# A decoder step's shared-value projection laid out by tokens, and two operand preparations moved, on one Trainium2 core

## The chip, the cores and the metric

The program runs on one core of one Trainium2 chip. A core has TensorE (PE: matrix products into the accumulation memory PSUM), VectorE (DVE), ScalarE (ACT), GpSimd (POOL), and SyncE (SP), which here only issues DMA transfers. Each engine works through its own instruction stream in order, and the streams meet through semaphores. The metric is the device time of one execution in microseconds (us); lower is better. Runs of one kernel are told by their median.

## The reference, cut to what matters

A two-layer decoder step over 512 prompt tokens and 32 sample tokens (8 sequences of 4), model width 1024, 8 heads of 128. Layer 0 is feed-forward, gated token mixing, feed-forward, gated embedding. From its output one shared key, value and log-forget are made, and layer 1 attends to them. All data are float32.

```python
def shared_kv(h, kv_norm, w_kvf, b_f, k_norm):
    xs = rmsnorm(h, kv_norm)
    kvf = xs @ w_kvf                                   # 1024 -> 1024 keys, 1024 values, 8 forgets
    k = rmsnorm(kvf[..., :D_ATT].reshape(bsz, L, N_HEADS, HEAD_DIM), k_norm)
    v = kvf[..., D_ATT:2 * D_ATT].reshape(bsz, L, N_HEADS, HEAD_DIM)
    logf = jax.nn.log_sigmoid((kvf[..., 2 * D_ATT:] + b_f).astype(jnp.float32))
    return k, v, logf
...
# layer 1
h = h + 0.5 * swiglu(rmsnorm(h, ffn1_norm[1]), ...)
xn = rmsnorm(h, mix_norm[1])
q = rmsnorm((xn @ att_w_q).reshape(bsz, L, N_HEADS, HEAD_DIM), q_norm)
o = fox_prompt(q, k, v, lf)          # causal softmax attention with a forget bias
h = h + o.reshape(bsz, L, D_ATT) @ att_w_o
h = h + 0.5 * swiglu(rmsnorm(h, ffn2_norm[1]), ...)
```

The keys, values and forgets are outputs too.

## The kernel before, in words

**Layout.** The activations lie transposed: features on the 128 partitions, all 544 tokens (512 prompt, then 32 sample) along the free dimension. A 1024-wide activation is 8 tiles of 128 x 544.

**Products in two parts.** Each float32 operand is split into a high part, which ACT casts (L192 for weights, L279 and L291 for activations), and a low part, which DVE subtracts (L193, L280, L292). A product is three TensorE matmuls: high x high, high x low, low x high (L235, L239, L241). In `mm` the weight block of 128 x 128 is the stationary operand and the 544 tokens move past it in two column ranges of 256 and 288, so one output tile of 128 features takes 8 blocks x 3 products x 2 ranges = 48 matmuls. The outputs go to the PSUM pool `ps`, three buffers of two banks; a second pool `pb` has two buffers of one bank. The large SBUF pool `big` has 45 buffers.

**Weights.** They come in pieces of 512 KB in a fixed order (`build` lists them). `unit` hands out the next piece and calls `prepare`, which splits up to two pieces ahead and loads up to four ahead; the load is issued on SP (L159) and the two split instructions go to ACT and DVE.

**Shared keys and values (`kv`).** One tile for the forgets; eight key tiles (evicted with the row scale `rstd` on DVE, squared on ACT L702, summed by heads with small float32 matmuls L710, then rsqrt on ACT L334 and DVE L337 to L341); then eight value tiles. The row scales of the keys go through DRAM (L721) and come back spread over the partitions (L726). Beside each value tile stand: its eviction on DVE (L765), its store (L766), the `v_turn` of the tile before (four float32 transposes L796 of 128 tokens and one for the sample tokens L797, then split and two stores L802, L803), a key's norm (`k_norm`), and `prep` of one tile of the next feed-forward's input. After value tiles 3 and 5 stands one `forms`.

**`forms`** makes four operands of the feed-forward's seven-product scheme from two input tiles: two ACT scalings (L301), three DVE differences (L305, L307, L308) and two splits (L279, L280), each waiting for the one before. The feed-forward takes four of them; those that are not there yet it makes itself beside its first four plain tiles.

**Projection after attention.** The output projection has its first half of the tokens done in `project_half` (L1172 to L1176, beside the heads), then `project(0)` to `project(7)` for the second half: 24 matmuls of 272 columns each, an add on DVE (L1196) and `on_chunk`, which makes the next input's `prep` and square, and, with `early=2`, a `forms` after chunks 1 and 3.

**Order.** In these two stages a scheduler at build time orders each engine's stream by its own time model, by the order in which the program names the steps where nothing else decides; in the feed-forward the order is written out by hand.

Of the kernel before, what the change touches and what calls it, by code (L numbers as in the profile page):

```python
# [22 lines left out]
F32 = mybir.dt.float32  # L23
# [6 lines left out]
P = 128  # L30
# [36 lines left out]

G_FFN1, G_MIX, G_FFN2, G_PLE = 0, 16, 32, 48
# [3 lines left out]
C_ID, C_ROLE, C_B4, C_H, C_SEL, C_NEGQ, C_TRI4 = 0, 128, 140, 144, 152, 156, 160  # L72
NCONST = 192
# [15 lines left out]
class Builder:  # L89
# [456 lines left out]
    def next_norm(self, h, gcol, early=0):  # L546
# [3 lines left out]
        def on_chunk(c, cols=slice(0, T)):  # L550
# [6 lines left out]
            if c % 2 and c // 2 < early and cols.stop == T:  # L557
                box["f"].append(self.forms(h, gcol, c // 2, self.pairs(box)))
        return on_chunk, box

# [170 lines left out]
    def kv(self, h, box, ffn_gain):  # L731
# [12 lines left out]
        for hh in range(NH):  # L744
            p = self.tile_mm(xs)
            if hh % 2 == 0:
                kt = self.big()

            def take(p=p, kc=kt[:, hh % 2, :]):
                nc.vector.tensor_tensor(kc, whole(p), rstd, ALU.mult)  # L750
                kraw.append(kc)
                sqs.append(self.square(kc))
            self.evac(take)
            if hh == 5:
                bcs += self.head_rows(sqs[:4])
            if hh >= 6:
                rows[hh - 6] = bcs[hh - 6]()
        vpend = None
        nxt = {"x": {}, "f": []}
        for hh in range(NH):  # L760
# [8 lines left out]
            vpend = (hh, vc)  # L769
            with self.tc.issue_after(last.ins):  # L770
                self.k_norm(hh, kraw, rows)
            if hh + 2 < NH:
                rows[hh + 2] = bcs[hh + 2]()
            nxt["x"][hh] = self.prep(h[hh], ffn_gain + hh)
            if hh in (3, 5):
                nxt["f"].append(self.forms(h, ffn_gain, len(nxt["f"]), self.pairs(nxt)))
        self.v_turn(*vpend)
# [12 lines left out]

    def v_turn(self, hh, vc):

        nc = self.nc
        t, ts = self.pb(), self.pb()
        for j in range(4):
# [621 lines left out]
```

## Time and profile before

| | |
|---|---|
| median of 3 runs | 2067.21 us (2066.38 to 2067.87) |
| profiled execution | 2068.19 us, of which 2066.4 us from the first to the last instruction |
| PE busy in the span | 2042.8 us (99%), 16388 matmuls |
| DVE, ACT, POOL busy | 1509.9 us (73%), 941.1 us (46%), 180.5 us (9%) |
| mean granted TensorE clock | 0.999 |
| `kv` stage, from its forget tile to the first seven-product matmul | about 974 to 1105 us |
| second half of the projection | about 1605 to 1635 us |

Matmuls overlap: one lasts longer than the distance to the next one's start. So the distance between the starts of neighbours tells what a matmul costs the stream, not its duration. What could be saved by waits alone is the span less the busy time, 23.6 us, of which 7.3 us lie at the very start.

### The profile page before, as it was taken

The numbers are of one execution on the slowest core, as the hardware profiler recorded it, in microseconds if no ns is written. First come the engines' busy times: TensorE is split into PE (matmuls) and PEld (weight loads), VectorE is DVE, ScalarE is ACT, GpSimd is POOL, SyncE is SP. The second block draws the span as 40 slices with busy tenths as digits, with TensorE's granted clock in tenths as the row PEclk, the third lists the DMA queues.
The fourth block names the chain that finished last, engine by engine and source line by source line (L and its number), as shares of the span: only waits on it lengthen the run. The fifth ranks groups of instructions, "written<-read, shape, count | busy, mean of one in ns | idle before, by whom it ended". The sixth has DMA issues, their size and how long they took to land.

```text
span 2066.4 us, 38759 instructions
## 1 busy us (share of the span) xinstructions
PE 2042.8 (99%) x16388; PEld 2015.9 (98%) x16388; DVE 1509.9 (73%) x1874; ACT 941.1 (46%) x1389; POOL 180.5 (9%) x230
## 2 busy tenths in 40 slices
PE   8999999999999999999999999999999999999999
PEld 8999999999999999999999999999987999999999
DVE  7877777556687778776698777786476878777773
ACT  6535344423554344454356344444374744344451
POOL 0000000400100000052050000001042200000020
PEclk9999999999999999999999999999999999999999
DMA  5233234212223232432184322323668332232421
GB/s 184 83 111 110 74 105 146 92 45 82 83 92 113 72 113 79 147 98 92 35 321 168 102 103 93 113 74 121 214 209 287 103 103 82 103 103 82 129 97 44
DMA packets 93887, 237.94 MB, mean 115 GB/s; under 512 B 9602, under 2 KB 27554, under 8 KB 93714
## 3 DMA queue, kind: packets, MB, share of 16 engines
q1 hardware_dynamic: 93570, 235.42, 33.9%
q8 instruction: 129, 2.11, 0.4%
q14 instruction: 44, 0.36, 0.1%
q10 hardware_dynamic: 144, 0.04, 0.0%
HBM read 218.94 MB, written 16.49 MB: 114 GB/s over the span
## 4 chain that ended last, share of the span: by engine, by line
PE 93%; DVE 3%; DMA 1%; ACT 1%; issue 1%; POOL 1%; SPq 0%; ACTq 0%; DVEq 0%; POOLq 0%
PE ps L485 33%; PE ps L235 16%; PE ps L241 16%; PE ps L239 16%; PE pb L485 6%; PE ps L1172 1%; PE ps L1176 1%; DVE big L193 1%; PE ps L1175 1%; ACT big L192 0%; PE ps L1129 0%; DMA tmp<-rows 0%; PE ps L623 0%; PE pb L1091 0%; POOL big L837 0%
## 5 line engine op out<-in xcount | busy, mean ns | idle before, releaser
L485 PE MATMUL ps<-big,big 128*128 128x272 f32 x5616 | 727.2, 288 | 0.7 <-DVE big L502 0.7
L485 PEld LDWEIGHTS ps<-big,big 128*128 128x128 f32 x5616 | 714.2, 189 | 0.9 <-issue 0.9
L193 DVE TENSOR_TENSOR big<-big,big 128x1024 fp32r<-128x1024 f32 (+2 forms) x538 | 590.1, 1099 | 108.8 <-ACT big L192 108.2
L192 ACT CAST big<-big 128x1024 fp32r<-128x1024 f32 (+2 forms) x538 | 488.4, 932 | 265.1 <-DVE big L178 260.4
L235 PE MATMUL ps<-big,big 128*128 128x256 f32 (+1 forms) x2832 | 590.5, 290 | 8.0 <-ACT big L192 7.3
L241 PE MATMUL ps<-big,big 128*128 128x256 f32 (+1 forms) x2832 | 585.1, 288 | 1.0 <-DVE big L193 1.0
L239 PE MATMUL ps<-big,big 128*128 128x256 f32 (+1 forms) x2832 | 585.0, 287 | 0.0
L235 PEld LDWEIGHTS ps<-big,big 128*128 128x128 f32 x2832 | 454.1, 189 | 10.3 <-ACT big L192 7.3
L239 PEld LDWEIGHTS ps<-big,big 128*128 128x128 f32 x2832 | 457.1, 189 | 0.0
L241 PEld LDWEIGHTS ps<-big,big 128*128 128x128 f32 x2832 | 453.4, 188 | 2.5 <-DVE big L193 2.1
L320 POOL TENSOR_TENSOR st<-st,tmp 128x544 f32<-128x544 f32 (+1 forms) x63 | 88.3, 1401 | 1619.2 <-ACT tmp L318 1619.0
L524 DVE SCALAR_TENSOR_TENSOR big<-ps,big 128x544 f32<-128x544 f32 x160 | 115.6, 723 | 106.6 <-PE ps L241 106.4
L178 DVE TENSOR_TENSOR big<-big,big 128x1024 f32<-128x1024 f32 x156 | 190.1, 1219 | 0.0
L493 ACT COPY tmp<-ps 128x544 f32<-128x544 f32 x117 | 71.7, 613 | 147.4 <-PE ps L485 147.4
L448 ACT ACTIVATE big<-big 128x544 f32<-128x544 f32 x88 | 58.0, 660 | 161.9 <-DVE big L445 160.7
L485 PE MATMUL pb<-big,big 128*128 128x272 f32 x936 | 124.0, 288 | 0.0
L445 DVE TENSOR_TENSOR big<-big,st 128x1088 f32<-128x1088 f32 x88 | 113.4, 1290 | 10.6 <-ACT big L507 8.9
L485 PEld LDWEIGHTS pb<-big,big 128*128 128x128 f32 x936 | 120.2, 189 | 0.0
L291 ACT ACTIVATE big<-big,gains 128x544 fp32r<-128x544 f32 (+1 forms) x80 | 56.0, 704 | 119.0 <-DVE big L524 64.9
L280 DVE TENSOR_TENSOR big<-big,big 128x544 fp32r<-128x544 f32 (+1 forms) x104 | 75.2, 726 | 28.3 <-ACT big L279 28.0
L292 DVE SCALAR_TENSOR_TENSOR big<-big,gains,big 128x544 fp32r<-128x544 f32 (+1 forms) x80 | 63.9, 805 | 26.6 <-ACT big L291 26.6
L279 ACT CAST big<-big 128x544 fp32r<-128x544 f32 (+1 forms) x104 | 66.7, 645 | 29.0 <-DVE big L784 15.2
(187 smaller groups left out, 1246.2 us busy)
## 6 DMA issues: line engine op xcount, KB each, us to landing
big<-in_w SPq DMA_DIRECT2D x156, 512.0 KB
big<-in_w2a SPq DMA_DIRECT2D x64, 512.0 KB
big<-in_w2b SPq DMA_DIRECT2D x32, 384.0 KB
big<-in_w13p SPq DMA_DIRECT2D x16, 512.0 KB
big<-in_win SPq DMA_DIRECT2D x16, 512.0 KB
big<-in_wg SPq DMA_DIRECT2D x16, 512.0 KB
big<-in_wkv SPq DMA_DIRECT2D x16, 512.0 KB
big<-in_ck SPq DMA_DIRECT2D x16, 512.0 KB
```

What stands on the lines that cost most here:

```text
L178: self.nc.vector.tensor_tensor(t, a, b, ALU.add if op == "+" else ALU.subtract)
L192: self.nc.scalar.copy(hi, src)
L193: self.nc.vector.tensor_tensor(lo, src, hi.bitcast(F32), ALU.subtract)
L235: i = nc.tensor.matmul(out[:, a:b], wh, xh[:, a:b], start=s, stop=False)
L239: nc.tensor.matmul(out[:, a:b], wh, xl[:, a:b], start=False, stop=False)
L241: nc.tensor.matmul(out[:, a:b], wl, xh[:, a:b], start=False, stop=e)
L280: self.nc.vector.tensor_tensor(pair[:, 1, cols], src, pair[:, 0, cols].bitcast(F32), ALU.subtract)
L320: nc.gpsimd.tensor_tensor(acc[:, cols], acc[:, cols], sq, ALU.add)
L445: tt(g, g, rstd.unsqueeze(1).broadcast_to([P, 2, T]), ALU.mult)
L485: nc.tensor.matmul(dst[w], a[:, c], b, start=k in "152" and kp == 0 and n == 0, stop=kp == NKP - 1 and n == 2, skip_group_check=True)
L493: nc.scalar.copy(t["r" + k], t["C" if k == "5" else "A"])
L524: nc.vector.scalar_tensor_tensor(h[c], whole(out), 0.5, h[c], ALU.mult, ALU.add)
```

## The change

Three edits.

1. `next_norm` takes a table of chunks for its `forms`. The token mixer's table gives what it had. The projection's `forms` 0 and 1 move from chunks 1 and 3 to chunks 5 and 6.
2. The values are computed with tokens on the partitions. The activation's 128 tokens are now the stationary operand, and 512 output columns (four heads) of the weights move: per weight piece `u` 4 token groups x 2 blocks x 3 products = 24 matmuls of 512 columns, with four pieces to a half. The two `ps` buffers of a half stay open over its four pieces. The 32 sample tokens are computed in plain float32 from the raw weights, four blocks side by side in 32 columns of the array each, after every second piece. `columns` turns the row scale into a column once; 16 ACT copies scale and evict the prompt's values; two matmuls (`sample_sums`) add the four partial sums of the sample rows. The transposes and `v_turn` go.
3. A written order, `KV_ORDER`, mixes key tiles (k), value pieces (v), head statistics (s), row reads (r), key norms (n), `prep` (p), `forms` (f), value stores (w) and the columns (c); the weight pieces are loaded in that order.

```diff
+KV_ORDER = """
+k0 k1 c0 k2 k3 k4 s0 k5 r0 r1 v0 n0 r2 k6 n1 r3 k7 n2 p0 s1 v1 n3 p1 r4 r5 v2 n4 r6 p2 v3 n5 r7 p3 f0
+v4 n6 w0 p4 v5 n7 w0 p5 v6 f1 p6 v7 p7 w0 w0
+"""
...
-            if c % 2 and c // 2 < early and cols.stop == T:
-                box["f"].append(self.forms(h, gcol, c // 2, self.pairs(box)))
+            if c in early and cols.stop == T:
+                box["f"].append(self.forms(h, gcol, early[c], self.pairs(box)))
...
+    def raw_sample(self, h, gcol, x):
+        for c in range(NC_):
+            self.nc.gpsimd.tensor_scalar(x[:, c, :], h[c][:, SEQ:], self.gain(gcol + c), None, ALU.mult)
+        return x
...
+    def columns(self, rstd):
+        nc, t = self.nc, self.pb()
+        for j in range(4):
+            nc.tensor.matmul(t[:, j:j + 1], rstd[:, j * P:(j + 1) * P], self.ident[:, 0:1], start=True, stop=True)
+        for j in range(4):
+            nc.tensor.matmul(t[32 * j:32 * j + 32, 4:5], rstd[:, SEQ:], self.ident[:, 0:1], start=True, stop=True,
+                             skip_group_check=True)
+        rc = self.sm(5)
+        nc.scalar.copy(rc, t[:, 0:5])
+        return rc
...
+    def token_half(self, xs, xraw, half, u):
+        hi, lo = self.unit()
...
+        if u == 0:
+            half["p"] = self.ps(), self.ps()
...
+        for i in range(4):
+            t, out = slice(i * P, i * P + P), half["p"][i // 2][:, i % 2, :]
+            for a in range(2):
+                k, c = 2 * u + a, slice(512 * a, 512 * a + 512)
+                xh, xl = xs[k]
+                nc.tensor.matmul(out, xh[:, t], hi[:, c], start=k == 0, stop=False)
+                nc.tensor.matmul(out, xh[:, t], lo[:, c], start=False, stop=False)
+                nc.tensor.matmul(out, xl[:, t], hi[:, c], start=False, stop=k == NC_ - 1)
+        if u % 2:
+            if u == 1:
+                half["s"] = self.pb()
+            for n in range(4):
+                k = 2 * u - 2 + n
+                nc.tensor.matmul(half["s"][32 * n:32 * n + 32, :], xraw[:, k, :], half["r"][k], start=k < 4, stop=k >= 4,
+                                 skip_group_check=True)
+
+    def sample_sums(self, sv, half):
+        t = self.pb()[:NS, :]
+        self.nc.tensor.matmul(t, self.c[:, C_SUM:C_SUM + NS], sv[:, 512 * half:512 * half + 512], start=True, stop=True)
+        return t
...
-        for hh in range(NH):
-            p = self.tile_mm(xs)
-            if hh == 0:
-                bcs += self.head_rows(sqs[4:])
-            vc = self.tmp()
-            last = nc.vector.tensor_tensor(vc, whole(p), rstd, ALU.mult)
-            nc.sync.dma_start(out=o["v"][hh], in_=vc)
-            if vpend is not None:
-                self.v_turn(*vpend)
...
+        def v_step(n):
+            g, u = divmod(n, 4)
+            self.token_half(xs, xraw, half, u)
+            if u < 3:
+                return
...
+            for i in range(4):
+                for a in range(2):
+                    nc.scalar.activation(
+                        vs[a][:, :, i], half["p"][i // 2][:, i % 2, 256 * a:256 * a + 256].rearrange(
+                            "p (h d) -> p h d", h=2), AF.Copy, scale=rc[:, i:i + 1])
+            nc.scalar.activation(sv[:, 512 * g:512 * g + 512], half["s"], AF.Copy, scale=rc[:, 4:5])
...
+        def v_store(_):
+            for hh, x in box["v"][:2]:
+                pair = self.big(F32R)
+                nc.sync.dma_start(out=o["v"][hh], in_=x)
+                self.split_pair(pair, x, slice(0, SEQ))
+                nc.sync.dma_start(out=self.vd[hh], in_=pair[:, :, :SEQ].bitcast(F32))
...
-    def v_turn(self, hh, vc):
-        t, ts = self.pb(), self.pb()
-        for j in range(4):
-            nc.tensor.transpose(t[:, j * P:(j + 1) * P], vc[:, j * P:(j + 1) * P], self.ident)
-        nc.tensor.transpose(ts[:NS, :P], vc[:, SEQ:], self.ident)
-        pair = self.big(F32R)
-        self.split_pair(pair, t, slice(0, SEQ))
...
-        on, nxt = self.next_norm(h, G_FFN2, early=3)
+        on, nxt = self.next_norm(h, G_FFN2, early={1: 0, 3: 1, 5: 2})
...
-        on, nxt = self.next_norm(h, G_FFN2 + 8, early=2)
+        on, nxt = self.next_norm(h, G_FFN2 + 8, early={5: 0, 6: 1})
```

The value output for the prompt is stored as 128 tokens x (group, feature) per head; the sample rows are one output of their own.

## Rows read from the trace of the kernel before

**Rows 1.** The page's busy times, shares of the span and instruction counts by engine.

```profile
PE 2042.8 (99%) x16388; PEld 2015.9 (98%) x16388; DVE 1509.9 (73%) x1874; ACT 941.1 (46%) x1389; POOL 180.5 (9%) x230
```

**Rows 2.** PE's waits over the span: us in total, times, longest us.

```profile
PE ps L1172 <- ACT big L192: 2.2, 1, 2.2
...
PE ps L241 <- DVE big L193: 1.0, 2, 0.5
PE ps L1176 <- DVE big L193: 0.7, 1, 0.7
```

**Rows 3.** Windows in the projection: us; PE, PEld, DVE, ACT, POOL busy; clock; DMA.

```profile
1616.00:1620.00 4.00, 1.88 (x16) 1.66 (x14) 3.46 (x7) 2.56 (x5) 0.92 (x1) 1.00 0.45 142
1620.00:1624.00 4.00, 3.19 (x14) 2.98 (x15) 3.92 (x4) 2.98 (x6) 0.99 (x1) 0.67 0.31 117
...
1628.00:1632.00 4.00, 4.00 (x34) 4.00 (x34) 4.00 (x5) 2.90 (x6) 1.82 (x2) 1.00 0.34 131
```

**Rows 4.** PE's timeline around that stretch: start, duration, instruction, idle before.

```profile
1617.59 0.29 PE L1176 MATMUL ps<-big,big 128*128 128x272 f32 x1
1620.06 0.39 PE L1172 MATMUL ps<-big,big 128*128 128x272 f32 x1 [2.19 <-ACT big L192]
...
1624.84 0.29 PE L1176 MATMUL ps<-big,big 128*128 128x272 f32 x1
```

**Rows 5.** The chain that ended last, same stretch: start, us, what.

```profile
1617.46 0.94 DVE tmp L308
1618.42 0.38 ACT big L279
...
1618.97 1.05 ACT big L192
```

**Rows 6.** PE's timeline over the last key tiles: head sums, then 72 plain pairs.

```profile
1011.24 0.41 PE L241 MATMUL ps<-big,big 128*128 128x256 f32 x2
1011.58 1.12 PE L710 MATMUL pb<-tmp,ones 128*32 128x272 f32 x16
...
1012.99 0.41 PE L239 MATMUL ps<-big,big 128*128 128x256 f32 x2
...
1030.42 0.41 PE L241 MATMUL ps<-big,big 128*128 128x256 f32 x2
```

**Rows 7.** PE's timeline around one value head's transposes.

```profile
1037.65 0.41 PE L241 MATMUL ps<-big,big 128*128 128x256 f32 x2
1037.90 0.60 PE L796 MATMUL pb<-consts,tmp 128*128 128x128 f32 x4
...
1038.70 0.42 PE L239 MATMUL ps<-big,big 128*128 128x256 f32 x2
```

**Rows 8.** PE's timeline in attention: four 512-column matmuls, and the next one.

```profile
1509.35 0.40 PE L1012 MATMUL ps<-big,big 128*128 128x512 f32 x1
...
1510.28 0.28 PE L1020 MATMUL ps<-neg,identr 128*128 128x256 f32 x1
```

**Rows 9.** PE's timeline over 24 float32 matmuls of 512 columns in 32-column strips.

```profile
1588.46 1.91 PE L1129 MATMUL ps<-big,tmp 128*32 128x512 f32 x12
...
1594.14 0.39 PE L1172 MATMUL ps<-big,big 128*128 128x272 f32 x1
```

**Rows 10.** PE's timeline in the queries: head sums of one late head.

```profile
1475.86 1.10 PE L710 MATMUL pb<-tmp,ones 128*32 128x272 f32 x4
```

**Rows 11.** PE's timeline in the token mixer: four float32 matmuls, and what follows.

```profile
455.17 1.06 PE L623 MATMUL ps<-big,big 128*128 128x128 f32 x8
456.16 0.40 PE L626 MATMUL ps<-tmp,big 32*128 32x32 f32 x2
```

**Rows 12.** A window in the value tiles, columns as in rows 3.

```profile
1053.00:1059.00 6.00, 6.00 (x51) 5.99 (x50) 5.34 (x6) 3.71 (x7) 5.00 (x5) 1.00 1.05 397
```

**Rows 13.** The chain at the start of the next feed-forward.

```profile
1091.26 5.57 DMA big<-in_w
```

**Rows 14.** ACT's timeline: two evictions of 272 columns from PSUM.

```profile
1012.36 0.92 ACT L334 ACTIVATE st<-pb,eps 128x272 f32<-128x272 f32 x2 [0.82 <-PE pb L710]
```

More of the change, by code (lines that the diff above doesn't have):

```diff
@@ L743, in kv, with k_tile, take @@
         sqs, bcs, rows = [], [], {}
-        for hh in range(NH):
+        nxt = {"x": {}, "f": []}
+        box, half, sv = {}, {}, self.flat(1024)
+        xraw = self.small.tile([P, NC_ * NS], F32, tag="xraw", name="xraw", bufs=1)[:].rearrange("p (c t) -> p c t", t=NS)
+        self.raw_sample(h, G_KV, xraw)
+        def k_tile(hh):
             p = self.tile_mm(xs)
             if hh % 2 == 0:
-                kt = self.big()
-            def take(p=p, kc=kt[:, hh % 2, :]):
-                nc.vector.tensor_tensor(kc, whole(p), rstd, ALU.mult)
+                box["k"] = self.big()
+            def take(p=p, kc=box["k"][:, hh % 2, :]):
+                box["last"] = nc.vector.tensor_tensor(kc, whole(p), rstd, ALU.mult)
                 kraw.append(kc)
@@ new lines, in v_store, with cols, stats, row @@
+        def v_store(_):
[4 more added lines that the diff above has]
+                nc.sync.dma_start(out=self.vd[hh], in_=pair[:, :, :SEQ].bitcast(F32))
+            del box["v"][:2]
+        def cols(_):
+            box["rc"] = self.columns(rstd)
+        def stats(a):
+            bcs.extend(self.head_rows(sqs[4 * a:4 * a + 4]))
+        def row(hh):
+            rows[hh] = bcs[hh]()
@@ new lines, in norm, with prep, forms @@
+        def norm(hh):
+            with self.tc.issue_after(box["last"].ins):
+                self.k_norm(hh, kraw, rows)
+        def prep(c):
+            nxt["x"][c] = self.prep(h[c], ffn_gain + c)
+        def forms(n):
+            nxt["f"].append(self.forms(h, ffn_gain, n, self.pairs(nxt)))
+        do = dict(k=k_tile, v=v_step, w=v_store, c=cols, s=stats, r=row, n=norm, p=prep, f=forms)
+        for step in KV_ORDER.split():
+            do[step[0]](int(step[1:]))
+        vs = self.big()[:NS, :, :512]
@@ L778, in kv @@
+        for a in range(2):
+            nc.scalar.copy(vs[:, a, :], self.sample_sums(sv, a))
+        nc.sync.dma_start(out=o["vs"].rearrange("t (a n) -> t a n", a=2), in_=vs)
+        nc.sync.dma_start(out=self.vsd[:].rearrange("t (a n) -> t a n", a=2), in_=vs)
         return nxt, rstd
@@ L1223, in build @@
         ple_units(0)
-        plain([i["wf"]] + [i["wkv"][c] for c in range(2 * NC_)])
+        plain([i["wf"]] + [i["w" + x[0]][int(x[1])] for x in KV_ORDER.split() if x[0] in "kv"])
         self.ffn_pieces(2)
@@ L1408, in rows @@
         return t[:SEQ], t[SEQ:]
-    y, k, v = rows(got["y"]), rows(got["k"]), rows(got["v"])
+    y, k = rows(got["y"]), rows(got["k"])
+    v = got["v"].reshape(NH, P, 4, P).transpose(2, 1, 0, 3), got["vs"]
     lf = got["lf"][::NQ].T
```

41 lines of the change are left out of this document (16 added, 25 removed).

## Prediction

> **What bounds the kernel now.** I read the page's busy times first: PE is busy for 99% of the span and no other engine for more than three quarters [rows 1]. So only two things can move the end: fewer or cheaper matmuls, and PE's few waits. The list of PE's waits gives the second. Apart from the very start it holds only short entries, and four of them lie where the change works: 2.2 us on a weight's high part and 0.7 us on a low part in the projection, and two of 0.5 us on low parts at the values [rows 2]. Then I read the timeline around the longest and the chain through it, and last the distances between starts of neighbouring matmuls, which are the prices for edit 2.
>
> **Edit 1, the projection's forms.** The last matmul of chunk 3 starts at 1617.59; the 18th of chunk 4 starts at 1624.84 [rows 4]. Those 18 steps take 7.25 us. A step of 272 columns is half a pair of 256 and 288. From 1012.99 to 1030.42 there are 70 pairs, so a pair costs 0.249 us, and 18 half pairs cost 2.24 us [rows 6]. The place loses 5.0 us. Some 2.9 us of it is the two waits [rows 2]. [...]
>
> What was late is the weight's high part, cast by ACT at 1618.97. ACT had been standing before a cast of `forms` (L279) that waited for the third difference of `forms` on DVE (L308, from 1617.46) [rows 5]. ACT works in order, so the weight's cast could not pass. With `forms` 0 after chunk 5 this cast has only `prep` and squares beside it, and the wait and the slow clock should go.
>
> What is late next? Both `forms` land between 1626 and 1640, where DVE is already full: 4.00 of 4 us in the window from 1628 [rows 3]. But the work behind them has more time: the four plain tiles of the next feed-forward take 4 x 24 pairs = 23.9 us before the first product that needs any of the four `forms`, and the first plain tile's weight is needed only when chunks 6 and 7 are through, about 6 us after chunk 5 (48 steps of 0.1245 us). I take back 4.6 us and leave 0.4 for a short wait there. Ends: 5.0 us back, or nothing if the jam only moves.
>
> **Edit 2, the matmuls of the values.** Removed: 8 tiles x 24 pairs x 0.249 = 47.8 us. Four transposes, the sample transpose and two pairs stand between 1037.65 and 1038.70, so the transposes of a head cost 1.05 - 0.50 = 0.55 us, eight heads 4.4 us [rows 7]. Together 52.2 us.
>
> Added: 192 matmuls of 512 columns. In attention four of these take 0.93 us, 0.2325 us each [rows 8]: 44.6 us. So the prompt's part gains 3.2 us, mainly because 512 columns pass where 544 did.
>
> The sample rows in plain float32: 16 matmuls of 512 columns, four side by side in strips of 32 columns. The nearest row has exactly this form: 24 such matmuls between 1588.46 and 1594.14, six rounds of four, 0.947 us a round [rows 9]. Going into this form and back costs extra. The head sums are eight such matmuls of 272 columns, two rounds: from 1011.24 to 1012.99, less two pairs, they take 1.25 us [rows 6]; two rounds scaled to 272 columns are 1.01 us, so a visit costs 0.25 us. The four groups stand at four places: 4 x (0.95 + 0.25) = 4.8 us; if the scheduler joins two groups, 4.3.
>
> `sample_sums`: two float32 matmuls in one strip, so one after the other. That strips in use matter, not matmuls, shows in the queries, where two matmuls of one late head take 1.10 us, as long as sixteen instructions do [rows 6, 10]. 2 x 0.95 + 0.25 = 2.1 us.
>
> `columns`: four float32 matmuls of full width and four narrow ones, one moving column each. The nearest row has 128 moving columns: four matmuls take 0.99 us [rows 11]. That is the upper end for the wide ones; with the visit and the narrow ones 1.5 us. The lower end is a visit alone, 0.25. I take 1.2, near the upper end, because the stationary load stays the same size.
>
> `s1`: the written order puts the second head sums right after key tile 7, whose own square cannot be ready. In the queries, with the same order of steps, one head came later by itself for 1.10 us [rows 10], where before both visits of `kv` took all eight together [rows 6]. I add 1.2 us; nothing if the stream is kept whole, 2.4 us if two heads come apart.
>
> Sum: 44.6 + 4.8 + 2.1 + 1.2 + 1.2 = 53.9 against 52.2, so 1.7 us more for PE.
>
> [...]
>
> **Edit 2 and 3, the other engines.** Sixteen evictions of 256 columns go to ACT. The nearest row is 0.46 us for 272 columns [rows 14], 7.4 us over the stage, and ACT is busy for 3.71 of 6 us there, so it is hidden [rows 12]. DVE loses eight evictions and is the engine with least room (5.34 of 6 us), so the two waits of 0.5 us on low parts [rows 2] should go: 1.0 us back.
>
> New waits: a half keeps two of the three `ps` buffers, so key tile 7 needs the buffer that tile 6 has just filled. The price is an eviction: 0.46 us by rows 14, some 1.3 us with the 0.82 us idle in front of it, or nothing if the scheduler runs a value piece there. The second half needs the first half's buffers after 12 matmuls (2.8 us), while their four evictions take 1.8 us. I take 0.7 us for both; ends 0 and 2. The bytes stay the same; `raw_sample` gives POOL eight small steps with nothing behind them that is late.
>
> So `kv` comes out at 1.7 - 1.0 + 0.7 = 1.4 us more, with ends of -2.4 (joined groups, whole sums, a cheap `columns`, all waits gone) and +5.5.
>
> **Total.** -4.6 + 1.4 = -3.2 us. The profiled execution took 2068.19 us (span 2066.4), 1.0 above the median of the runs, and would take 2065.0; for the median, 2067.2 - 3.2 = 2064.0 us.
>
> **The rivals.**
>
> *The jam moves.* `forms` 0 and 1 hold the casts of the next feed-forward's first weights or its last `prep`, as they held chunk 4's. For it: DVE is full there [rows 3]. Against it: 6 us of matmuls stand between. A wait half as long as the old, without the clock's fall, costs 1.5 us; the whole, 5.0. With the 1.4 us of `kv` the total is between -2.1 and +1.4: 2065.1 to 2068.6.
>
> *The values gain too.* Groups are joined, `s1` stays whole, the waits on low parts go and none comes: `kv` at -1 to -2.4, total -5.6 to -7.4: 2060 to 2061.6.
>
> *Slower: a weight comes late behind the value stores.* The last four heads' stores are issued after piece 7 on the SP queue that also issues weight loads. Each store waits for its cast and its low part; a load behind them waits too. DMA is at 1.05 in this stage [rows 12], and a load took 5.6 us to land [rows 13]. The last evictions and four splits take some 9 us (nine of 0.46, four of 1.3, an estimate from rows 14 and from rows 5's cast of 1.05 with its low part), the load 5.6, its split 2: 17 us, against 23.9 us of plain tiles. It decides from 7 us more on. Each microsecond of a wait there would cost up to 1.7, by the 5.0 us for 2.9 us of waits in the projection; 4.5 us late gives some 7.7 us, total +4.5: 2071.7 or more.
>
> *No effect*, below 0.5 us each way, would need edit 1's recovery to equal edit 2's cost by chance; it lies inside the first two cases.
>
> **How the numbers follow.** The forecast (-2.1 to -5.5 us) gets 0.50, the jam that moves 0.19, the values' gain 0.20, the late weight 0.11. Measurement tells about 0.2%, 4.1 us, from no change. Faster by more: the values' gain 0.20 and the forecast's lower part, 0.19: 0.39. Within: 0.31 of the forecast and 0.19: 0.50. Slower: 0.11. The range leaves out the late weight and the last few of the best cases: 2060.0 to 2069.0. The likeliest case's own is 2061.7 to 2065.1.
>
> **What would show it.** Right: no wait above 0.3 us at chunk 4, granted clock 1.00 from 1600 to 1640, 512-column matmuls 0.23 us apart, four sample groups near 1.2 us each. Wrong: a PE wait at the next feed-forward's first tile or at key tile 7, sample matmuls scattered one by one among others (each then costs a whole round), or 512-column steps away from 0.2325.

## The result and the profile after

The changed kernel took 2073.46 us (median of 10 runs, 2072.14 to 2074.43), the kernel before 2067.68 us beside it (10 runs). The ratio is 1.0027, with an interval of 1.0019 to 1.0035: slower by about 5.6 us, or 5.8 between the medians, where 3.2 us less were forecast and the range ended at 2069.0. The profiled execution has a span of 2071.9 us (before 2066.4).

The page's busy times, to be held against [rows 1]:

```profile
PE 2046.5 (99%) x16208; PEld 2002.1 (97%) x16208; DVE 1506.4 (73%) x1866; ACT 947.8 (46%) x1402; POOL 183.5 (9%) x238
```

PE has 180 matmuls fewer and is busy for 3.7 us longer. (The trace has two records for each plain float32 matmul, sixteen for the eight head sums of [rows 6], and its counts, here and below, are of records.) To see where the time went, I cut each trace at three matmuls: the last 272-column group ahead of `kv`, the first one behind it, and the last matmul of the projection. The table is made of the starts that PE's timelines show there, in us; its first stretch also holds some 100 us of work ahead of `kv`, and "rest" goes to the kernel's last matmuls. It has the experiments too, which are told below; "time-before" is the median against that of the kernel before in the same comparison, while the stretches are of the one profiled execution, which can lie some 1 us from the median.

```
kernel                  time-before  kv stage  to end of projection  rest
before                      -         238.7         529.7           427.0
after                     +5.8        246.0         525.0           430.0
e1 forms alone            -2.3        238.5         525.1           430.0
e2 values alone           +8.9        245.8         530.6           427.0
e3 sums whole             -1.3        240.6         522.8           430.5
e4 keys first             -0.4        239.6         525.4           430.0
e5 norms later            +4.3        244.7         524.3           430.0
e6 sums, norms            -0.8        241.0         522.3           430.5
e7 sums, form 1 and 6     +1.3        241.6         528.5           427.0
e8 no sample              -1.1        240.2         523.2           430.5
e9 no row wait            +0.3        240.8         525.1           430.0
e10 sums, form 4 and 5    +1.3        240.5         523.3           432.5
e11 sums, no early form   -1.5        240.5         522.6           430.2
e12 before, sums, forms   -3.8        238.8         522.2           430.0
e13 one form              -4.8        238.5         523.7           427.4
e14 sums, norms at v6     -0.8        240.9         522.4           430.5
e15 sums, no row wait     -2.0        240.4         522.5           430.4
```

So three things happened. `kv` grew by 7.2 us (forecast 1.4). The stretch with the projection shrank by 4.7 (forecast 5.0). And the last stretch, with the next feed-forward, grew by 3.1 (forecast 0.4). Together they are the 5.6 us.

**The projection.** Windows of the changed kernel, columns as in [rows 3]:

```profile
1616.00:1620.00 4.00, 4.00 (x34) 4.00 (x34) 3.69 (x5) 2.91 (x5) 0.63 (x1) 1.00 0.15 48
1620.00:1624.00 4.00, 4.00 (x34) 4.00 (x34) 4.00 (x6) 2.68 (x7) 0.81 (x1) 1.00 0.38 128
```

PE is busy throughout these windows, the clock is 1.00, and the wait on the weight's high part at chunk 4 is gone: the jam of [rows 2 to 5] was read rightly. But the next network's first tile now waits (PE's timeline):

```profile
1643.38 0.52 PE L241 MATMUL ps<-big,big 128*128 128x256 f32 x2 [0.18 <-ACT big L198]
1644.64 0.52 PE L247 MATMUL ps<-big,big 128*128 128x256 f32 x2 [0.49 <-DVE big L199]
```

Two more waits of 0.5 us follow, at 1675.44 and 1682.22.

**The `kv` stage.** The second head sums stood in one visit of sixteen records before the change, like the first ones in [rows 6] (PE's timeline of before):

```profile
1030.76 1.12 PE L710 MATMUL pb<-tmp,ones 128*32 128x272 f32 x16
```

They came apart into four visits, one head each (PE's timeline after; L769 was L710):

```profile
1018.18 1.10 PE L769 MATMUL pb<-tmp,ones 128*32 128x272 f32 x4
...
1025.39 1.10 PE L769 MATMUL pb<-tmp,ones 128*32 128x272 f32 x4
...
1038.17 1.10 PE L769 MATMUL pb<-tmp,ones 128*32 128x272 f32 x4
...
1044.96 1.10 PE L769 MATMUL pb<-tmp,ones 128*32 128x272 f32 x4
```

And PE waits at value piece v4 (PE's timeline):

```profile
1061.03 0.49 PE L603 MATMUL ps<-big,big 128*128 128x512 f32 x1 [2.53 <-ACT big L198]
1062.49 0.50 PE L603 MATMUL ps<-big,big 128*128 128x512 f32 x1 [0.97 <-ACT big L829]
...
1063.42 0.63 PE L603 MATMUL ps<-big,big 128*128 128x512 f32 x1
...
1065.98 0.63 PE L603 MATMUL ps<-big,big 128*128 128x512 f32 x1
...
1066.93 0.39 PE L603 MATMUL ps<-big,big 128*128 128x512 f32 x1
1067.16 0.39 PE L604 MATMUL ps<-big,big 128*128 128x512 f32 x1
```

That is 3.5 us of standing still; then six steps from 1063.42 to 1065.98 take 0.427 us each at a granted clock of 0.50, where the step is 0.23 at the 1.00 granted from 1066.93 to 1070. By the count of matmuls (24 to a piece, 36 from 1046.00 to the wait), half of v4 was through by then. By the same count the matmul at 1061.03 is the first of the next piece, whose weight is cast at 1059.95. The one at 1062.49 begins v4's second half and waits for a buffer of the values' first half, which ACT evicts (L829). I keep the name "the wait at v4" for both. The windows (columns as in [rows 3]) show a lower granted clock, and ahead of it DVE and ACT almost idle:

```profile
1053.00:1059.00 6.00, 5.49 (x35) 1.68 (x34) 1.02 (x2) 0.23 (x1) 0.20 (x1) 1.00 0.31 124
1059.00:1065.00 6.00, 3.01 (x8) 2.23 (x9) 4.61 (x6) 6.00 (x14) 3.48 (x5) 0.84 0.93 315
```

[Rows 12] had 5.34 and 3.71 us busy in the first of these windows. What the two stood at is told by their own waits: DVE's from 990 to 1112, then ACT's from 1052 to 1062.

```profile
DVE big L877 <- DMA tmp<-rows: 5.3, 2, 4.7
```

```profile
ACT big L285 <- DVE big L877: 7.1, 1, 7.1
```

L877 is a key norm of the second group, L285 the first split behind it. The chain of work that ended last shows what these norms wait for, behind the last head sum at 1044.96:

```profile
1049.85 1.74 DVE tmp L343
...
1051.69 0.80 DVE tmp L346 x2
...
1052.51 0.74 DVE st L347
...
1053.30 1.16 DMA rows<-st
...
1054.99 4.29 DMA tmp<-rows
...
1059.30 0.74 ACT big L297
1060.04 0.93 ACT big L198
```

The rows of the reciprocal roots go out to memory and come back spread over the partitions: the first is there at 1057.95, 4.7 us after the last step on DVE (L347), the one in this chain after 6 us. DVE and ACT work in order and stand at the norms that need the rows. Behind them stand the cast of the next weight (L198) and the eviction of the first half (ACT's timeline), though the last matmul of that half had started at 1051.43:

```profile
1060.88 3.01 ACT L829 ACTIVATE big<-ps,sm 128x256 f32<-128x256 f32 x8
```

### The profile page after: what moved, and what is told of

It reads as the page before. It is cut to its first block, busy times and chain, and to the rows that moved or that the text cites. A ratio compares the mean times of both kernels' runs of the same rounds, so it can differ in the third digit from the quotient of the medians.

```text
span 2071.9 us, 38393 instructions
## 1 busy us (share of the span) xinstructions
PE 2046.5 (99%) x16208; PEld 2002.1 (97%) x16208; DVE 1506.4 (73%) x1866; ACT 947.8 (46%) x1402; POOL 183.5 (9%) x238
## 4 chain that ended last, share of the span: by engine, by line
PE 92%; DVE 4%; ACT 2%; issue 1%; DMA 1%; SPq 0%; POOL 0%; DVEq 0%; ACTq 0%
PE ps L491 33%; PE ps L241 16%; PE ps L247 16%; PE ps L245 16%; PE pb L491 5%; DVE big L199 1%; ACT big L198 1%; PE ps L1251 1%; PE ps L1255 1%; PE ps L1254 1%; DMA tmp<-rows 1%; PE ps L1208 0%; DVE big L286 0%; ACT big L285 0%; DVE big L184 0%
## 5 line engine op out<-in xcount | busy, mean ns | idle before, releaser
L491 PEld LDWEIGHTS ps<-big,big 128*128 128x128 f32 x5616 | 714.2, 188 | 2.4 <-issue 1.6
L199 DVE TENSOR_TENSOR big<-big,big 128x1024 fp32r<-128x1024 f32 (+2 forms) x538 | 592.5, 1103 | 107.1 <-ACT big L198 106.4
L198 ACT CAST big<-big 128x1024 fp32r<-128x1024 f32 (+2 forms) x538 | 488.0, 931 | 267.6 <-DVE big L184 262.8
L241 PE MATMUL ps<-big,big 128*128 128x256 f32 (+1 forms) x2704 | 562.7, 289 | 7.4 <-ACT big L198 7.4
L247 PE MATMUL ps<-big,big 128*128 128x256 f32 (+1 forms) x2704 | 558.5, 288 | 1.5 <-DVE big L199 1.5
L245 PE MATMUL ps<-big,big 128*128 128x256 f32 (+1 forms) x2704 | 558.0, 287 | 0.0
L241 PEld LDWEIGHTS ps<-big,big 128*128 128x128 f32 x2704 | 433.4, 189 | 10.0 <-ACT big L198 8.3
L247 PEld LDWEIGHTS ps<-big,big 128*128 128x128 f32 x2704 | 432.8, 188 | 3.2 <-DVE big L199 2.7
L245 PEld LDWEIGHTS ps<-big,big 128*128 128x128 f32 x2704 | 435.9, 189 | 0.0
L286 DVE TENSOR_TENSOR big<-big,big 128x544 fp32r<-128x544 f32 (+1 forms) x112 | 80.5, 727 | 28.9 <-ACT big L285 28.8
L298 DVE SCALAR_TENSOR_TENSOR big<-big,gains,big 128x544 fp32r<-128x544 f32 (+1 forms) x80 | 66.7, 840 | 28.6 <-ACT big L297 28.6
L285 ACT CAST big<-big 128x544 fp32r<-128x544 f32 (+1 forms) x112 | 71.0, 645 | 22.5 <-DVE big L877 9.0
```

Of the source, the lines that this page charges most:

```text
L198: self.nc.scalar.copy(hi, src)
L199: self.nc.vector.tensor_tensor(lo, src, hi.bitcast(F32), ALU.subtract)
L241: i = nc.tensor.matmul(out[:, a:b], wh, xh[:, a:b], start=s, stop=False)
L245: nc.tensor.matmul(out[:, a:b], wh, xl[:, a:b], start=False, stop=False)
L247: nc.tensor.matmul(out[:, a:b], wl, xh[:, a:b], start=False, stop=e)
L286: self.nc.vector.tensor_tensor(pair[:, 1, cols], src, pair[:, 0, cols].bitcast(F32), ALU.subtract)
```

## The experiments

In what is on record ahead of the runs, F is the forecast, J that the jam moves to the next network, K that `kv` carries the loss by its split sums and its wait. Later, W and W2 stand for the wait for the rows, X for a lack of time on vector and scalar engine that only moves a wait. The runs e8, e9, e13 and e15 leave out or replace work that the result needs: they price a cause and are no versions to use.

**The two edits apart.** e1 is the kernel before with the new table for the projection, e2 the changed kernel with the old one.

```diff
-        on, nxt = self.next_norm(h, G_FFN2 + 8, early={1: 0, 3: 1})
+        on, nxt = self.next_norm(h, G_FFN2 + 8, early={5: 0, 6: 1})
```

> The kernel before with edit 1 alone (forms 0 and 1 of the projection after chunks 5 and 6). Theory J (the jam moves): the trace after has no wait at chunk 4 but four waits of 0.2 to 0.5 us on weights and sums at the start of the next feed-forward, so the 5.0 us come back and some 3 are lost: 2.0 us faster than before (1 to 3). Rival F (the forecast): the late waits belong to the changed kv stage in front of it, and alone the move gives 4 to 5 us.

Measured: 2065.93 us against 2068.18, ratio 0.999 (0.9981 to 0.9999).

> The changed kernel with the projection's forms back at chunks 1 and 3, so edits 2 and 3 alone. Theory K (all of the loss, and more, is in kv): the start of the next feed-forward comes 7.2 us later than before, so this runs 7 to 8 us slower than before, some 2 us slower than the changed kernel. Rival: the two edits disturb each other, and this runs within 1 us of the changed kernel or faster.

Measured: 2077.03 us, ratio 1.0041 (1.0027 to 1.0055). The edits are separate, as J had it, and K but for its size (7 to 8 us): in e1 the projection's stretch gives back 4.6 us and the rest takes 3.0, with `kv` as before; in e2 `kv` grows by 7.0 and the projection's stretch by 0.9. Alone they are worth -2.3 and +8.9 us, together 6.6, where the changed kernel has 5.8; e2 has five runs, 2073.8 to 2077.5 us. The first edit is worth 2 us, not 4.6, and the second costs all that was lost and more.

**The head sums kept whole** (e3): the changed kernel, with the last head's sum issued first and the others behind it.

```diff
-            for j, sq in enumerate(sqs):
-                self.nc.tensor.matmul(pbs[a][32 * j:32 * j + 32, :HT], self.ones,
+            for j, sq in reversed(list(enumerate(sqs))):
+                with ExitStack() as s:
+                    if whole and first is not None:
+                        s.enter_context(self.tc.issue_after(first.ins))
+                    i = self.nc.tensor.matmul(pbs[a][32 * j:32 * j + 32, :HT], self.ones,
```

> The changed kernel with the second head sums issued as one group behind the last head's first matmul: one visit in place of four. Theory K1 (the split visits cost PE 3 x 1.25 us, the wait for the late key rows another 5.1 with the slow clock, and the two add up): 3.75 us faster than the changed kernel (3 to 4.5), with the wait before value piece 4 still there. Rival K2 (only the row round trip sets the pace, and the visits fill time that would be waited): the wait grows by what the visits save, and the time stays within 1 us of the changed kernel.

Measured: 2066.89 us, ratio 0.9996 (0.9987 to 1.0005), 6.6 us less than the changed kernel. The sums are one visit again (PE's timeline), four microseconds earlier than the last of the four:

```profile
1040.99 1.12 PE L772 MATMUL pb<-tmp,ones 128*32 128x272 f32 x16
```

More came back than four visits cost, which neither K1 (3 to 4.5 us) nor K2 (under 1 us) had, and in two places. `kv` is 5.3 us shorter: 3.1 by the visits (32 head-sum records take 2.1 us of PE's stream instead of 5.2, both groups), the rest by a shorter wait at v4, with steps of 0.23 us behind it. PE's waits there:

```profile
PE ps L603 <- ACT big L198: 1.6, 1, 1.6
...
PE ps L603 <- ACT big L833: 1.0, 1, 1.0
```

And the turned order joined the queries' sums too, from five visits to two, which I had not meant; the middle stretch is 2.2 us shorter with it.

**All key tiles ahead of the values** (e4):

```diff
-k0 k1 c0 k2 k3 k4 s0 k5 r0 r1 v0 n0 r2 k6 n1 r3 k7 n2 p0 s1 v1 n3 p1 r4 r5 v2 n4 r6 p2 v3 n5 r7 p3 f0
-v4 n6 w0 p4 v5 n7 w0 p5 v6 f1 p6 v7 p7 w0 w0
+k0 k1 c0 k2 k3 k4 s0 k5 k6 r0 k7 r1 v0 s1 n0 r2 p0 v1 n1 r3 p1 v2 n2 r4 p2 v3 n3 r5 p3 f0 v4 n4 r6 w0 p4
+v5 n5 r7 w0 p5 v6 n6 f1 p6 v7 n7 p7 w0 w0
```

> The changed kernel with another order: all key tiles first, the second head sums after value piece 0, a key's norm beside each value piece (edit 2 without edit 3's mixing). Theory K (loss = split sums 3.75 + late rows 5.1): one visit, rows early, no wait before value piece 4: 7 to 9 us faster than the changed kernel, 1.5 to 3.5 us faster than before. Rival S (the float32 sample matmuls, their sums and the two held PSUM buffers are the loss): less than 4 us of it comes back, still 1.5 us or more slower than before.

Measured: 2067.74 us, ratio 0.9997 (0.9988 to 1.0006): 5.7 us less than the changed kernel, between what the two theories named. The second sums are whole and stand 14 us earlier, at 1030.91. No value piece waits. But one of the next network's first tiles does, for its weight (PE's timeline); the window from 1089 to 1095 was granted 0.79 of the clock:

```profile
1092.04 0.52 PE L241 MATMUL ps<-big,big 128*128 128x256 f32 x2 [2.20 <-ACT big L198]
```

**The norms behind the value pieces** (e5: changed kernel, split sums; e6: with whole sums). A row that comes late should then hold back nothing that PE needs soon.

```diff
-... v2 n4 r6 p2 v3 n5 r7 p3 f0 v4 n6 w0 p4 v5 n7 w0 p5 v6 f1 p6 v7 p7 w0 w0
+... v2 r6 p2 v3 r7 p3 f0 v4 w0 p4 n4 v5 n5 w0 p5 n6 v6 n7 f1 p6 v7 p7 w0 w0
```

> The changed kernel with the order of kv's steps altered in one respect: the norms of key heads 4 to 7, which wait for rows that come back through memory, stand behind the value pieces v4 to v6 and their stores instead of before them (v4, then n4, v5, n5 and so on). The second head sums are still made in four visits. Theory W (the rows of the second key group come late, and the norm that waits for them on the vector engine holds back the weight's form of v4, 3.5 us of wait and about 1.6 us of half clock behind it): 4 to 5 us faster than the changed kernel, 2068.5 to 2069.5 us, no wait over 1 us at v4. Rival X (the weight is late because vector and scalar engine are too full there, whatever the order): the wait only moves to v5 or to the next key tiles, under 1.5 us faster than the changed kernel, 2072 us or more.

Measured: 2072.04 us, ratio 1.002 (1.0011 to 1.0029): 1.4 us less than the changed kernel, as rival X had it. PE's timeline shows where the wait went, a later piece:

```profile
1072.52 0.80 PE L604 MATMUL ps<-big,big 128*128 128x512 f32 x1 [2.68 <-DVE big L199]
```

The window from 1071 to 1077 was granted 0.56 of the clock. DVE still stood 6.3 us at two norms for their rows, only with other work behind it.

> Both repairs at once: all head sums issued as whole groups (which in the run before joined the queries' sums too) and the norms of key heads 4 to 7 behind the value pieces. Theory W, with the two losses separate: 2.5 to 3.5 us faster than the run with whole sums alone (2066.9), so 2063.4 to 2064.4 us, faster than the kernel before. Rival X: the wait moves, not under 2066 us.

Measured: 2066.88 us, ratio 0.9996 (0.9987 to 1.0005): nothing beside whole sums alone. Theory W, that placing these norms later is enough, fell.

**The sample tokens' products left out** (e8): whole sums, no 32-column float32 matmuls.

```diff
-                nc.tensor.matmul(half["s"][32 * n:32 * n + 32, :], xraw[:, k, :], half["r"][k], start=k < 4, stop=k >= 4,
-                                 skip_group_check=True)
...
-            nc.scalar.activation(sv[:, 512 * g:512 * g + 512], half["s"], AF.Copy, scale=rc[:, 4:5])
+            nc.gpsimd.memset(sv[:, 512 * g:512 * g + 512], 0.0)
```

> Whole head sums, and the added value products of the 32 sample tokens left out: the 32-column float32 matmuls and the copy of their result; zeros stand for their sums, so the sample tokens' values and all that follows from them are not computed. Forecast's term: these matmuls cost 4.8 us of a busy engine, so 4 to 5 us faster than whole sums alone (2066.9), 2062 to 2063 us. Rival H (they stand ahead of the late value piece v4 and fill its wait, so without them the wait grows by as much): under 1.5 us faster, 2065.4 us or more, with the wait at v4 grown from 2.6 us to 4 us or over.

Measured: 2066.61 us, ratio 0.9993 (0.9984 to 1.0002): no gain, as rival H had it. PE's wait at v4 ends 0.4 us later than its first part does in e3 (1056.47), and is longer:

```profile
1056.88 0.79 PE L603 MATMUL ps<-big,big 128*128 128x512 f32 x1 [5.52 <-DVE big L286]
```

So PE's own work ahead of v4 does not decide when this wait ends; the other two engines do. Another 1.1 us of what was saved went to this run's own edit: PE waits 1.15 us at 1058.82 for the memset on POOL.

**The wait for the rows taken away** (e9): the changed kernel, split sums and all, but norms 4 to 7 multiply by numbers long in place.

```diff
-        bc = rows.pop(hh)
+        bc = rows.pop(hh) if hh < 4 else rstd
```

> The changed kernel, but the norms of key heads 4 to 7 multiply by the layer's own reciprocal roots, which have long been in place, instead of the rows that come back through memory (so these four heads' keys are scaled by other numbers than the reference's); the second head sums and the rows' transfers are still made, in four visits as before, and nothing else is moved. Theory W2 (in every version so far the vector engine stands still for 5 to 6 us at the first of these norms, the forms behind it are late by as much, and the value piece or key tile that is next shows it): the wait before the value piece is gone, 3.5 to 5 us faster than the changed kernel (2073.5), 2068.5 to 2070 us. Rival X (vector and scalar engine lack the time in kv's second half, and the wait only moves): under 1.5 us faster, 2072 us or more, with waits of over 2.5 us elsewhere in kv's second half.

Measured: 2068.22 us, ratio 1.0001 (0.9992 to 1.001): 5.2 us less than the changed kernel, with the head sums still in four visits. PE's waits in `kv`, all that is left:

```profile
PE ps L247 <- DVE big L199: 1.0, 2, 0.5
PE ps L241 <- ACT big L198: 0.5, 1, 0.5
```

and the windows in which DVE had been busy for 1.02 us and PE for 3.01:

```profile
1053.00:1059.00 6.00, 6.00 (x35) 3.64 (x34) 4.91 (x6) 1.27 (x3) 2.03 (x2) 1.00 0.62 245
1059.00:1065.00 6.00, 6.00 (x32) 4.52 (x32) 3.77 (x7) 4.49 (x8) 0.35 (x1) 1.00 0.58 158
```

ACT's timeline in e9 has the evictions right behind the first half's matmuls, 10 us sooner than in the changed kernel:

```profile
1049.77 1.56 ACT L829 ACTIVATE big<-ps,sm 128x256 f32<-128x256 f32 x4
1052.09 1.57 ACT L829 ACTIVATE big<-ps,sm 128x256 f32<-128x256 f32 x4 [0.76 <-PE ps L605]
```

This is theory W2: about as much time as DVE spends standing at those norms (5.3 us) PE loses later. With no row to wait for, the planner also put the four norms forward, to 1040.28, so e9 prices the wait together with the place that it forced on the norms.

**Both taken away** (e15), **and one more order** (e14, norms one piece later than in e6).

> Whole head sums, and the norms of key heads 4 to 7 multiply by the layer's own reciprocal roots instead of rows from memory (these four heads' keys are scaled by other numbers than the reference's): both losses of the second head sums taken away. If the row wait (5.2 us) and the split visits (3.1 us in kv, some 2 us more in the queries) add up: 2063 to 2064 us. If the engine's work of the second half is what remains, so that one repair leaves nothing for the other: 2065.5 to 2067 us, like either repair alone.

Measured: 2065.90 us, ratio 0.9991 (0.9982 to 1.0), about 1 us less than whole sums alone, which is within the two intervals. The two losses do not add up. The four norms now come together, between 1037.6 and 1041.6, ahead of a weight's low part, and an earlier piece waits for that:

```profile
1045.25 0.50 PE L604 MATMUL ps<-big,big 128*128 128x512 f32 x1 [2.21 <-DVE big L199]
```

> Whole head sums, and the norms of key heads 4 to 7 behind value piece v5 in the order of kv's steps, one piece later than in the run with norms behind v4, so that the vector engine has the forms of v4 to v6 and two stores before the first of them. Theory W2: the rows have come when the vector engine gets there, no wait over 1 us at a value piece, 2 to 3 us faster than whole sums alone (2066.9): 2064 to 2065 us, with all that the reference asks for. Rival X (with the norms that late, the four norms, their splits and their stores press on the last pieces and on the next network's first tiles): a wait over 1 us there instead, 2066 us or more.

Measured: 2067.11 us, ratio 0.9995 (0.9986 to 1.0004): rival X again, with waits of 1.8 and 0.6 us at value pieces and 1.6 us at the next network's first tiles.

**The place of the projection's forms.** All with whole sums.

```diff
-        on, nxt = self.next_norm(h, G_FFN2 + 8, early={5: 0, 6: 1})
+        on, nxt = self.next_norm(h, G_FFN2 + 8, early={1: 0, 6: 1})   e7
+        on, nxt = self.next_norm(h, G_FFN2 + 8, early={4: 0, 5: 1})   e10
+        on, nxt = self.next_norm(h, G_FFN2 + 8, early={})             e11
```

> Whole head sums, and of the projection's two early forms the first back where it was before the change, behind chunk 1, the second left behind chunk 6. Theory J (each form is work of about 5 us on a vector engine that is full from the projection's second half to the start of the next network; only the second of two early forms makes the weight of chunk 4 late, and the first one moved back is taken off the start of the network): 1 to 2 us faster than whole sums alone (2066.9), 2065 to 2066 us, no wait over 0.6 us at chunk 4. Rival J2 (one early form is enough to make chunk 4's weight late, with the half clock behind it): 2067 us or more, with a wait over 1 us at chunk 4.

Measured: 2069.02 us, ratio 1.0005 (0.9996 to 1.0014), 2.1 us more than with chunks 5 and 6. One form behind chunk 1 is enough for the whole old wait at chunk 4, and the rest of the kernel then takes 427.0 us again, as before the change (PE's timeline):

```profile
1620.62 0.39 PE L1255 MATMUL ps<-big,big 128*128 128x272 f32 x1 [2.19 <-ACT big L198]
```

> Whole head sums, and the projection's two early forms one chunk sooner than in the changed kernel: behind chunks 4 and 5 instead of 5 and 6. Theory J (forms made before chunk 4's weight make that weight late, forms made after it only press on what comes next, and the sooner they are done the less of the start of the network): no wait at chunk 4, 0.5 to 1.5 us faster than whole sums alone (2066.9), 2065.4 to 2066.4 us. Rival J2 (they meet the weight of chunk 5 or 6 instead): a wait over 1 us there, 2067.5 us or more.

Measured: 2069.30 us, ratio 1.0006 (0.9997 to 1.0015). Chunk 4 does not wait, and the wait is at the next network's first tile instead, which neither text named:

```profile
1633.06 0.52 PE L241 MATMUL ps<-big,big 128*128 128x256 f32 x2 [2.97 <-ACT big L198]
```

> Whole head sums, and none of the four forms made early: all four stand behind the projection. Theory J (a form costs the vector engine about 5 us wherever it stands, and the start of the network has no cover for it): the start of the network loses 2 to 5 us more than with two early forms, 2069 to 2072 us. The forecast's view (the forms are covered by the network's first chunks, so moving them off the projection costs nothing): 2065 to 2067 us.

Measured: 2066.42 us, ratio 0.9997 (0.9988 to 1.0006), as with two early forms. J, as a price for each form at the start of the network, fell: four forms there lose the same 3 us as two. PE's waits from 1640 to 1700:

```profile
PE ps L491 <- ACT tmp L499: 1.8, 2, 0.9
...
PE ps L491 <- DVE big L508: 0.5, 1, 0.5
```

**Three forms left out** (e13): e1, where the last network's products take the first form in place of the other three.

```diff
+        if gcol == G_FFN2 + 8 and n:
+            half = lambda t, b: tuple(x[:, b * HT:(b + 1) * HT] for x in t)
+            return dict(self.form0, **{"1": half(xs[2 * n], 0), "2": half(xs[2 * n + 1], 0), "3": half(xs[2 * n + 1], 1)})
```

> The kernel before with the change's first edit alone (2065.9 when run with its own forms), and in the last network three of the four forms left out: the products take the first form's difference operands in their place, so this network's result is not the reference's, and neither scalar nor vector engine makes the other three. Theory J (the forms crowd the start of the network, which gives 3.0 of the 5.0 us back): the waits at the start of the network fall below 0.5 us in total, and 2 to 3 us come off, 2063 to 2064 us. Theory P (what is late there are the weights' own forms and the evictions, passed back and forth between scalar and vector engine, whatever the forms do; the run with no early form lost the same 3.0 us): 2065.2 us or more, with two waits of about 0.5 us near 1665 and 1675 us as before.

Measured: 2063.14 us, ratio 0.9974 (0.9964 to 0.9984). That is theory J's range. The list of PE's waits is empty from 1600 to 1700, and the rest takes 427.4 us, 2.6 less than in e1. So it is the forms' work that the start of the network pays for. Its place matters too: the rest takes 430 us with two early forms behind chunks 5 and 6 or none (e11), 432.5 behind 4 and 5 (e10), and 427.0 in e7, where the old wait at chunk 4 stands.

**The first edit and whole sums, values as before** (e12): e1 with e3's order of the head sums.

> The kernel before with the change's first edit only (the projection's forms behind chunks 5 and 6) and its head sums, the queries' too, issued as whole groups; values as before. If the two are separate, the first edit's 2.3 us and the 1.5 to 2.5 us that whole sums gave behind kv add up: 2063.0 to 2064.5 us, faster than both kernels. If the queries' visits are hidden by a later wait for the row sums' way through memory: 2065.5 us or more.

Measured: 2064.12 us, ratio 0.9982 (0.9973 to 0.9991): 3.8 us faster than the kernel before and 9.3 faster than the changed one, as forecast for two separate gains. `kv` is as before, the queries' sums are whole.

## Why the prediction was wrong

**Edit 1, first half: right.** The chain, the two waits and the low clock at chunk 4 (0.67 in [rows 3]) were what the forms cost, and 4.7 us came back there (4.6 in e1) of the 5.0 that were reckoned. In the trace of before the granted clock was 0.50 from 1621.68 to 1624.63, with 13 steps of 0.227 us, and 1.00 from 1624.84 to 1628, with steps of 0.125.

**Edit 1, "What is late next?": wrong.** I put the cover at four plain tiles, 23.9 us, and left 0.4 us for a short wait. The start of the next network lost 3.0 us, in e1 as in the changed kernel. That cover counts PE's work only. e13 shows what it left out: without three forms 2.6 of the 3.0 us are gone. My reading is that the stall at chunk 4 had also been time in which DVE and ACT made the forms, and that without it this work presses on the network's first weights and evictions. e7, where the stall stands and the start of the network loses nothing, fits; no run separates it from other readings. This is the rival "the jam moves", which I priced at 1.5 to 5.0 us and gave 0.19. Why four forms behind the projection cost no more than two (e11) stays open.

**Edit 2, the matmuls: nearly right, by errors that cancel.** The distances between the starts in `kv`, summed by kind, in us, before and in e9, which has the change without the row wait:

```
                              before    e9    change   forecast
128-row, 256 to 288 columns    226.1   176.3   -49.8    -47.8
transposes                       3.5     0      -3.5     -4.4
512 columns                      0      45.7   +45.7    +44.6
head sums                        2.1     5.2    +3.1     +1.2
sample products                  0       3.6    +3.6     +4.8
sample_sums                      0       1.9    +1.9     +2.1
columns                          0       1.05   +1.05    +1.2
sum                                             +2.0     +1.7
```

The 512-column steps are 0.231 us apart, as from [rows 8]; they stand here with what waits and changes of form fall between them (0.32 and 0.34 us for the steps ahead of and behind the sample products at 1057.28 in e9). The `s1` term was too small. It reckoned with one head that comes later by itself and, as an end, two; all four came by themselves, as their squares did, 9 to 13 us apart. The sample products were too dear, since they came in two visits of sixteen records instead of four of eight. Their price was not from one form either: of the program's 24 matmuls between the two ends of [rows 9], eight are of 32 rows (L1134), and those of 128 rows take 1.84 and 1.86 us for two rounds.

**"New waits", 0.7 us with ends of 0 and 2: the step that failed.** I looked for two waits on PE's own buffers. The one at key tile 7 did not come: the planner put it behind piece v1. The one of the second half for the first half's buffers did, but I had priced it by the length of four evictions, 1.8 us (1.57 in e9), and ACT's work as hidden by its busy time in [rows 12]. Those evictions and the next weight's cast were held back because ACT stood 7.1 us for a norm on DVE, and DVE for its row. The price was 5.2 us (e9), 3.5 of it in PE's waits and the rest in the clock behind them (0.50 from 1063.42 to 1065.98). I followed what the written order moves on PE and not where the second group's norms stand on DVE and ACT: their rows cannot be there until the last head sum, its roots, and a way out to memory and back (1.16 and 4.29 us) are through. Before the change the second group's sums came at 1030.76, ahead of the value tiles, and DVE had no such wait in the stage. The order puts key tile 7 behind a value piece; the planner put v1 there too, and v2 ahead of the last sum, whose square was done at 1039.76. So that sum came at 1044.96.

**The two waits on low parts, 1.0 us back: wrong.** Two such waits are there again, 0.49 and 0.47 us at 1099.27 and 1105.99, both on the next network's first tiles. Before, only one of the two lay at the values (1079.64); the other (1099.25) lay on those tiles, where this edit takes no work away.

**How far the explanation holds.** In the forecast's own terms `kv` is 2.0 us from the matmuls, nothing back on low parts and 5.2 from the new wait, which is the 7.2 us measured. The row wait is shown by e9. That the split sums cost 3.1 us of PE's stream is shown by their places. But the two do not add up (e15), norms placed later gain nothing (e6, e14), and less work on PE gains next to nothing (e8): with one repair or both `kv` takes between 240.2 and 241.6 us, and where the visits are saved a wait stands at some other piece or tile. This fits a second half of `kv` that goes by the order of work on DVE and ACT, of which PE shows whichever wait comes out; that is argued, and which order would be free of waits stays open. e4 came nearest, at 239.6. With the old values the stage takes 238.7, so no version tried made the values faster.

The rival with a weight late behind value stores on SP did not show: the loads of the next network's first tiles were not what PE waited for.

## What to carry to other kernels

When work is mixed into a new order, follow each in-order engine's queue past every instruction whose input comes from far away (here rows through memory, 6 us), and ask which short, urgent step stands behind it; the busy shares do not show it, the waits of DVE and ACT do. A stall that is removed may have been cover for other engines: before its time is taken back in full, count what they did in it and where that work goes. And sums that are cheap as one visit (here 1.12 us for sixteen records together, 1.10 for four alone) should be tied together in the code, not left to the planner: that and the first edit alone made the fastest version here that computes the whole result (e12).

## What the hardware showed beside this

In the changed kernel two of DVE's instructions with both operands in SBUF took about twice their time beside one of POOL's that also has two (L916): 2.31 us against a median of 1.22 (L199) and 1.80 against 0.78 (L298). DVE's timeline in the changed kernel, then POOL's:

```profile
1029.47 1.22 DVE L199 TENSOR_TENSOR big<-big,big 128x1024 fp32r<-128x1024 f32 x1
...
1038.28 0.72 DVE L814 TENSOR_TENSOR big<-ps,st 128x544 f32<-128x544 f32 x1 [1.89 <-PE ps L247]
...
1045.82 1.80 DVE L298 SCALAR_TENSOR_TENSOR big<-big,gains,big 128x544 fp32r<-128x544 f32 x1
1047.55 2.31 DVE L199 TENSOR_TENSOR big<-big,big 128x1024 fp32r<-128x1024 f32 x1
```

```profile
1037.99 1.26 POOL L916 TENSOR_TENSOR big<-big 128x512 f32<-128x512 f32 x1
...
1041.25 9.75 POOL L916 TENSOR_TENSOR big<-big 128x512 f32<-128x512 f32 x5
```

L814, which reads one operand from PSUM, took 0.72 us beside L916, and 0.66 to 0.73 in all its eight places. L916 itself took 1.26 us at 1037.99 and 1.95 each for the five from 1041.25 on. Three slowed instructions (L298, L199 and L343 at 1.80, against a median of 0.73), each 1 us longer, lie between the last head sum and the rows, so L343 starts at 1049.78, though ACT's step ahead of it ended at 1046.60. That alone does not make the row wait: in e3 the three take 0.77, 1.21 and 0.71 us there (of the later steps L347 is slowed, to 1.63), and DVE still stands 4.5 and 0.9 us for the rows. What makes the slowing, and what it adds to the changed kernel's time, no run shows. The first line has POOL's one-input copy beside it, which starts 0.15 us after L199; L199 takes 1.22 us there.
